# A hybrid attention, convolution and mixture-of-experts layer: router steps, output weights, gated sums and two norms are put in another order and on other engines

## The chip, the cores and the metric

The kernel runs on one core of a Trainium2 chip. The core has five engines that work side by side and wait for each other through semaphores: TensorE (PE, matrix products into PSUM), VectorE (DVE), ScalarE (ACT), GpSimd (POOL) and SyncE (SP, which issues most DMAs). Each engine takes its instructions strictly in the order in which they stand. The metric is the device time of one execution in microseconds; less is better.

## The reference, cut to what matters

One layer for 2048 tokens of 1024 features in float32:

```python
proj = x @ w_in                       # q, k, v, conv cb/cc/ch, two gates
attn = stick_breaking_attention(q, k, v)          # 8 heads of 64
branch_a = attn @ w_branch_a
branch_b = short_gated_conv(cb, cc, ch, conv_w) @ w_branch_b
gates = sigmoid(gate_logits + gate_bias)
mixed = (gate_a * branch_a + gate_b * branch_b) @ w_out
h = layer_norm(ALPHA * x + mixed, ln1_g, ln1_b)
ffn = hierarchical_moe(h)   # router: top 1 of 4 groups, top 2 of its 8 experts; SwiGLU experts
out = layer_norm(ALPHA * h + ffn, ln2_g, ln2_b)
```

## The kernel before

Products in float32 are made of three products of rounded halves: a tensor is split into a high part (ScalarE, line 103, `split`) and a low part (VectorE or GpSimd subtracts the high part, line 109), and TensorE runs high x high, high x low, low x high. So almost every weight passes through ScalarE and VectorE.

The program runs in stages. Projections and attention fill the first half (line 168 and lines 291 to 336). Then, for groups of 512 tokens in the order 2, 3, 0, 1, come `branches` and `mix_norm`.

`branches` (line 471) runs eight steps m for a group. A step loads 512 KB of branch weights (`raw`, line 480) and 512 KB of gates (`gt`, line 485, two buffers), splits the weights into `wh` and `wl`, and runs 24 matmuls of 512 columns into two PSUM tiles `ps_p` (line 490; two buffers in all). VectorE multiplies each PSUM tile by its gate (line 493), GpSimd adds the two halves (line 494), and the sum is split into `mh` and `ml`, eight of which are kept for a group.

`load_wo` (line 548) loads one of eight 512 KB rows of the output weights and splits it; the odd ones have their low part on GpSimd. Their raw tiles share four buffers named `r` with other tiles. The eight loads are written behind group 2's branches, and a scheduler that works ahead of time places them.

`mix_norm` (line 578) multiplies by the output weights (lines 589 to 591), adds the residual (592) and calls `layer_norm` (433): statistics on VectorE (423, 424), a power on GpSimd (427), and then either three instructions on ScalarE, GpSimd and VectorE (439 to 441) or, "at once", two on VectorE (436, 437). Before, only the last tile of all is done at once.

`router` transposes a normed tile (607), splits it (`ht`) and multiplies it by the router's weights (612). `choose` ranks a group's tokens: transposes of the logits (639), some thirty small VectorE instructions, a prefix sum (674, 675), one-hot rows on GpSimd (451) and columns on VectorE (452), and products of both (711). TensorE's order is written out by hand up to here: the generator `branches` yields once per matmul, and the group loop runs a step of the router or of `choose` at fixed counts k of these yields, 0 to 191, of the next group. The other engines' orders are the scheduler's.

After the experts (lines 770 to 900) the second norm runs over 16 tiles of 128 tokens: loads of 512 KB (1136), then for each pair of tiles statistics, a power (427), and ScalarE, GpSimd and VectorE instructions (1170 to 1172), and for one pair two VectorE instructions a tile (1167, 1168). The gain `g2` is kept in SBUF and in PSUM, the bias `b2` in PSUM.

Of the kernel before, what the change touches and what calls it, by code (L numbers as in the profile page):

```python
# [26 lines left out]
NT = S // P  # L27
# [4 lines left out]
ALPHA = 2.0 ** 0.25  # L32
EPS = 1e-5
# [23 lines left out]
def tile_hybrid_layer(  # L57
# [40 lines left out]
    def f32(t):  # L98
        return t.bitcast(F32)
# [316 lines left out]
    def norm_scales(pool, rows, eps, shift=True):  # L416

        n = len(rows)
        mv = pool.tile([P, n, 2], F32, name="mv", bufs=LEAD + 2)
# [5 lines left out]
        rs = pool.tile([P, n, 2], F32, name="rs", bufs=LEAD + 2)  # L425
# [42 lines left out]
    ph_b1, ph, ph_w = ExitStack(), ExitStack(), ExitStack()  # L468
    bq = open_pool(ph_b1, "bq", 1, side="right")

    def branches(n, outs):
        ah = bq.tile([P, 2, 4, G], F32R, name="ah")
        yh = bq.tile([P, 2, 4, G], F32R, name="yh")
        for t, src in ((ah, a_d), (yh, y_d)):
            for b in range(4):
                nc.sync.dma_start(f32(t)[:, :, b, :], src[b][n].rearrange("t p f -> p t f"))
        yield PAUSE_2
        for m in range(8):
            raw = bq.tile([P, NC, P], F32, name="raw", bufs=2)
            nc.sync.dma_start(raw, w_ab[m])  # L480
            wh = bq.tile([P, NC, P], F32R, name="wh", bufs=2)
            wl = bq.tile([P, NC, P], F32R, name="wl", bufs=2)
            split(wh, wl, raw)
            gt = bq.tile([P, 2, G], F32, name="gt", bufs=2)
            nc.sync.dma_start(gt, g_d[m][n].rearrange("s p f -> p s f"))
            for s, src in ((0, ah), (1, yh)):
                ps = ps_p.tile([P, G], F32, name="ps_p")
                for c in range(4):
                    for k, (a, b) in enumerate(((wh, 0), (wh, 1), (wl, 0))):
                        nc.tensor.matmul(ps, lhsT=a[:, 4 * s + c, :], rhs=src[:, b, c, :],  # L490
                                         start=(c == 0 and k == 0), stop=(c == 3 and k == 2))
                        yield G
                nc.vector.tensor_tensor(gt[:, s, :], gt[:, s, :], ps, op=ALU.mult)
            nc.gpsimd.tensor_tensor(gt[:, 0, :], gt[:, 0, :], gt[:, 1, :], op=ALU.add)
            h = bq.tile([P, G], F32R, name="mh", bufs=8)
            l = bq.tile([P, G], F32R, name="ml", bufs=8)
            split(h, l, gt[:, 0, :])
            outs.append((h, l))

    br_2 = []  # L500
    mixed(late, branches(2, br_2), RATE_3)
    run(late)
    ph_at.close()

# [34 lines left out]
    if True:  # L539
# [40 lines left out]
        def mix_norm(n, i, mh, ml):  # L580
            t = n * 4 + i
            tk = slice(i * P, (i + 1) * P)
            r = bp.tile([P, D], F32, name="r", bufs=4)
            nc.sync.dma_start(r, x[t * P:(t + 1) * P, :])
            for f in range(2):
                fs = slice(f * G, (f + 1) * G)
                ps = ps_b.tile([P, G], F32, name="ps_b")
                for c in range(NC):
                    nc.tensor.matmul(ps, lhsT=mh[c][:, tk], rhs=wo_h[:, c, fs], start=(c == 0), stop=False)
                    nc.tensor.matmul(ps, lhsT=mh[c][:, tk], rhs=wo_l[:, c, fs], start=False, stop=False)  # L590
                    nc.tensor.matmul(ps, lhsT=ml[c][:, tk], rhs=wo_h[:, c, fs], start=False, stop=(c == NC - 1))
                nc.vector.scalar_tensor_tensor(r[:, fs], r[:, fs], ALPHA, ps, op0=ALU.mult, op1=ALU.add)
                if f == 0:
                    yield None
            layer_norm(bp, r, g1, b1, r, EPS, n == GROUPS[-1] and i == 3)
            nc.sync.dma_start(h_d[t * P:(t + 1) * P, :], r)
            nc.sync.dma_start(acc_d[t * P:(t + 1) * P, :], r)
            yield r
# [31 lines left out]
        def choose(t0, nt, lt):  # L630
# [73 lines left out]
            for h in range(0, 2 * nt, 4):  # L704
                hs = range(h, min(h + 4, 2 * nt))
                c1 = bp.tile([P, 4, 3, 2 * NE], F32R, name="r", bufs=4)
                for a in hs:
                    one_hots(r1[:, a, :], c1[:, a % 4], row[:, a:a + 1], col[:, a:a + 1], tva[:, a, :],
                             nc.vector if t0 // 4 == GROUPS[-1] else nc.gpsimd)
                for a in hs:  # L710
                    nc.tensor.matmul(ps_tab[:, 0:6 * NE], lhsT=r1[:, a, :], rhs=c1[:, a % 4],
                                     start=(t0 == 4 * GROUPS[0] and a == 0), stop=(t0 == 4 * GROUPS[-1] + 2 and a == 3))
                yield

        for c in range(NC):
# [412 lines left out]
    with ExitStack() as ph:  # L1128
# [22 lines left out]
                                 start=True, stop=True)  # L1151
        g2 = fp.tile([P, D], F32, name="g2", bufs=1)
        nc.scalar.activation(g2, g2_ps, AF.Copy)
        scales = {}
        for u in range(0, NT + 2 * LEAD, 2):
            if u < NT:
                load_rows(2)
                scales[u] = norm_scales(fp, rows[u:u + 2], EPS / ALPHA ** 2, u not in AT_ONCE)
            t = u - 2 * LEAD
            if t < 0:  # L1160
                continue
            pair, at_once = rows[t:t + 2], t in AT_ONCE
            mv, rs = scales[t]
            for k, r in enumerate(pair):
                o = fp.tile([P, D], F32, name="o")
                if at_once:
                    nc.vector.scalar_tensor_tensor(r, r, mv[:, k, 0:1], g2, op0=ALU.subtract, op1=ALU.mult)
                    nc.vector.scalar_tensor_tensor(o, r, rs[:, k, 0:1], b2, op0=ALU.mult, op1=ALU.add)  # L1168
                else:
                    nc.scalar.activation(r, r, AF.Identity, bias=rs[:, k, 1:2], scale=rs[:, k, 0:1])  # L1170
                    nc.gpsimd.tensor_tensor(r, r, g2, op=ALU.mult)
                    nc.vector.tensor_tensor(o, r, b2, op=ALU.add)  # L1172
                nc.sync.dma_start(out[(t + k) * P:(t + k + 1) * P, :], o)
# [45 lines left out]
```

## Time and profile before

| what | value |
|---|---|
| median of three runs (lowest, highest) | 2606.8 us (2599.53, 2611.36) |
| the profiled execution, its own time | 2614.91 us |
| its span in the trace | 2613.2 us |
| granted TensorE clock, mean over the span | 0.973 |
| TensorE busy with matmuls | 94% |
| VectorE, ScalarE, GpSimd busy | 69%, 52%, 37% |
| DMA read and written | 394.5 MB, 104.4 MB |

A share of busy time is a mean over the whole span. Where a stage could be shorter is read from the rows of that stage: which engine stands idle there, and what ended its wait. An interval in brackets behind a row of the timeline is the engine's idle time just before it, with the instruction or transfer that ended it.

### The profile page before, as it was taken

The numbers are of one execution on the slowest core, as the hardware profiler recorded it, in microseconds if no ns is written. First come the engines' busy times: TensorE is split into PE (matmuls) and PEld (weight loads), VectorE is DVE, ScalarE is ACT, GpSimd is POOL, SyncE is SP. The second block draws the span as 40 slices with busy tenths as digits, with TensorE's granted clock in tenths as the row PEclk, the third lists the DMA queues.
The fourth block names the chain that finished last, engine by engine and source line by source line (L and its number), as shares of the span: only waits on it lengthen the run. The fifth ranks groups of instructions, "written<-read, shape, count | busy, mean of one in ns | idle before, by whom it ended". The sixth has DMA issues, their size and how long they took to land. (4 is left out here: it accounts for less than half of the span.)

```text
span 2613.2 us, 36756 instructions
## 1 busy us (share of the span) xinstructions
PE 2467.8 (94%) x12724; PEld 2079.0 (80%) x12724; DVE 1803.7 (69%) x2655; ACT 1363.2 (52%) x2334; POOL 975.7 (37%) x1323
## 2 busy tenths in 40 slices
PE   8999999999999999999989999959999999999981
PEld 7878888888888888888778778748988888888870
DVE  3257876577866567666766575578788878887848
ACT  3245565455555556555532122136677767777642
POOL 0033443254444444444532232313342443343336
PEclk9999999999999999999999999969999999999995
DMA  7433464423233335332573564257899989998967
GB/s 262 145 106 112 135 202 154 154 89 101 81 117 108 99 105 175 104 105 69 182 286 131 201 213 142 97 209 252 286 310 318 324 302 325 321 316 295 306 175 259
DMA packets 195120, 501.38 MB, mean 192 GB/s; under 512 B 19921, under 2 KB 44497, under 8 KB 194929
## 3 DMA queue, kind: packets, MB, share of 16 engines
q1 hardware_dynamic: 182962, 456.91, 50.7%
q0 software_dynamic: 11968, 42.08, 6.9%
q8 instruction: 101, 1.65, 0.3%
q14 instruction: 89, 0.73, 0.1%
HBM read 394.52 MB, written 104.40 MB: 191 GB/s over the span
## 5 line engine op out<-in xcount | busy, mean ns | idle before, releaser
L168 PE MATMUL ps_p<-xh,wh 128*128 128x512 f32 x1280 | 504.9, 394 | 8.0 <-ACT xh L103 6.6
L168 PE MATMUL ps_p<-xh,wl 128*128 128x512 f32 x1280 | 503.3, 393 | 0.0
L168 PE MATMUL ps_p<-xl,wh 128*128 128x512 f32 x1280 | 503.1, 393 | 0.1
L316 POOL TENSOR_TENSOR w<-w,pi 128x512 f32<-128x512 f32 (+2 forms) x256 | 300.4, 1174 | 222.7 <-DVE pi L311 221.7
L311 DVE TENSOR_TENSOR_SCAN pi<-z,cr,w 128x512 f32<-128x512 f32 x192 | 246.2, 1282 | 197.8 <-ACT z L298 188.4
L296 ACT ACTIVATE w<-z 128x512 f32<-128x512 f32 (+1 forms) x320 | 170.4, 532 | 359.9 <-PE z L291 324.4
L109 DVE TENSOR_TENSOR wlo<-wraw,whi 128x1024 fp32r<-128x1024 f32 x256 | 313.6, 1236 | 39.8 <-ACT whi L103 38.3
L882 PE MATMUL pg<-xt,whi 128*128 128x384 f32 (+2 forms) x1216 | 333.7, 354 | 4.7 <-DVE v L888 4.6
L103 ACT ACTIVATE whi<-wraw 128x1024 fp32r<-128x1024 f32 x256 | 268.5, 1056 | 73.8 <-DMA wraw<-in_w_gu 68.0
L884 PE MATMUL pg<-xt,wlo 128*128 128x192 f32 (+2 forms) x1216 | 295.0, 243 | 0.0
L168 PEld LDWEIGHTS ps_p<-xh,wh 128*128 128x128 f32 x1280 | 241.1, 188 | 58.7 <-ACT xh L103 6.6
L168 PEld LDWEIGHTS ps_p<-xl,wh 128*128 128x128 f32 x1280 | 241.0, 188 | 51.3 <-DVE xl L109 0.6
L168 PEld LDWEIGHTS ps_p<-xh,wl 128*128 128x128 f32 x1280 | 241.0, 188 | 51.1
L882 PEld LDWEIGHTS pg<-xt,whi 128*128 128x128 f32 x1216 | 230.7, 190 | 7.5 <-DVE v L888 6.5
L884 PEld LDWEIGHTS pg<-xt,wlo 128*128 128x128 f32 x1216 | 234.6, 193 | 0.8
L109 DVE TENSOR_TENSOR wl<-raw,wh 128x1024 fp32r<-128x1024 f32 x112 | 177.8, 1587 | 75.0 <-ACT wh L103 70.8
L336 PE MATMUL acc<-wt,vt 128*128 128x512 f32 (+3 forms) x640 | 207.2, 405 | 1.7 <-DVE wt L109 1.0
L109 DVE TENSOR_TENSOR wt<-pt,wt 128x512 fp32r<-128x512 f32 (+1 forms) x320 | 188.1, 589 | 28.6 <-ACT wt L103 28.3
L103 ACT ACTIVATE wh<-raw 128x1024 fp32r<-128x1024 f32 x112 | 118.6, 1059 | 140.8 <-PE ps_p L168 84.9
L291 PE MATMUL z<-kt,qs 128*128 128x512 f32 (+3 forms) x640 | 180.7, 364 | 1.5 <-ACT stay L298 0.9
L109 DVE TENSOR_TENSOR dlo<-draw,dhi 128x1024 fp32r<-128x1024 f32 x96 | 117.2, 1235 | 93.7 <-ACT dhi L103 93.5
L103 ACT ACTIVATE dhi<-draw 128x1024 fp32r<-128x1024 f32 x128 | 132.6, 1056 | 90.4 <-DMA draw<-in_w_dn 60.9
(250 smaller groups left out, 4952.2 us busy)
## 6 DMA issues: line engine op xcount, KB each, us to landing
wraw<-in_w_gu SPq DMA_DIRECT2D x256, 512.0 KB, 6.8
draw<-in_w_dn SPq DMA_DIRECT2D x124, 512.0 KB, 6.9
raw<-in_w_in SPq DMA_DIRECT2D x80, 512.0 KB, 3.9
kt<-k_d SPq DMA_DIRECT2D x96, 256.0 KB, 3.9
g_d<-t SPq DMA_DIRECT2D x64, 256.0 KB, 2.0
raw<-in_w_ab SPq DMA_DIRECT2D x32, 512.0 KB, 3.5
gt<-g_d SPq DMA_DIRECT2D x32, 512.0 KB, 4.3
vt<-v_d SPq DMA_DIRECT2D x48, 256.0 KB, 3.2
```

The costliest lines, as they stand in the source:

```text
L103: nc.scalar.activation(hi, src, AF.Copy)
L109: eng.tensor_tensor(lo, src, f32(hi), op=ALU.subtract)
L168: nc.tensor.matmul(ps, lhsT=a[:, c, :], rhs=b[:, c, :], start=(c == 0 and k == 0), stop=(c == NC - 1 and k == 2))
L291: nc.tensor.matmul(z[:, lo:], lhsT=qs[:, i * P:(i + 1) * P], rhs=kt[:, t, lo:], start=(t == 0), stop=(t == 1))
L296: nc.scalar.activation(w[:, lo:], z[:, lo:], AF.Sigmoid, scale=DH ** -0.5)
L311: nc.vector.tensor_tensor_scan(pi[:, lo + 1:], stay[:, lo:], (stay if diag else w)[:, lo:], first, op0=ALU.mult, op1=ALU.bypass)
L316: eng.tensor_tensor(w[:, lo:], w[:, lo:], pi[:, lo:G], op=ALU.mult)
L336: nc.tensor.matmul(acc[:, 0:nq * P], lhsT=kv[h, kc][1][:, b, :], rhs=wt[:, s, 0:nq * P], start=(kc == j and b == 3 and s == 0), stop=(kc = ...
L882: nc.tensor.matmul(pg[:, 0:2 * cap], lhsT=wh[:, c, :], rhs=xt[:, c, :, :], start=(c == 0), stop=False)
L884: nc.tensor.matmul(pg[:, cap:2 * cap], lhsT=wl[:, c, :], rhs=xt[:, c, 0, :], start=False, stop=(c == NC - 1))
```

## The change

Five edits. The router's steps go to other counts k (8, 30, 42, 54, 132, 144, 168, 184 in place of 48, 66, 84, 150, 172, 188, and one that was run at once), and the one-hot rows are made a step earlier than their products. The split of branch weights of step m must stand behind the gate product of step m - 2 on its engines, and load c of the output weights behind the gate load of step c and the low part of step c - 1; all their low parts go to VectorE. The sum of the two gated halves goes from GpSimd to VectorE. The last tile of every group is normed at once. The second norm goes tile by tile, in four ways: statistics on VectorE ("v") or as two ScalarE sums ("s"), and the end on ScalarE, GpSimd and VectorE ("g") or on VectorE alone ("v").

```diff
@@ branches
+        merged = []
         for m in range(8):
...
-            split(wh, wl, raw)
+            with tc.issue_after(merged[-2].ins) if m > 1 else ExitStack():
+                split(wh, wl, raw)
             gt = bq.tile([P, 2, G], F32, name="gt", bufs=2)
-            nc.sync.dma_start(gt, g_d[m][n].rearrange("s p f -> p s f"))
+            asked = nc.sync.dma_start(gt, g_d[m][n].rearrange("s p f -> p s f"))
...
-                nc.vector.tensor_tensor(gt[:, s, :], gt[:, s, :], ps, op=ALU.mult)
-            nc.gpsimd.tensor_tensor(gt[:, 0, :], gt[:, 0, :], gt[:, 1, :], op=ALU.add)
+                gated = nc.vector.tensor_tensor(gt[:, s, :], gt[:, s, :], ps, op=ALU.mult)
+            merged.append(gated)
+            nc.vector.tensor_tensor(gt[:, 0, :], gt[:, 0, :], gt[:, 1, :], op=ALU.add)
...
-            split(h, l, gt[:, 0, :])
+            nc.scalar.activation(h, gt[:, 0, :], AF.Copy)
+            low = nc.vector.tensor_tensor(l, gt[:, 0, :], f32(h), op=ALU.subtract)
             outs.append((h, l))
+            if paced is not None:
+                paced.append((asked, low))
@@ load_wo, mix_norm, choose
-            split(wo_h[:, c, :], wo_l[:, c, :], raw, lo_eng="pool" if c % 2 else "dve")
+            split(wo_h[:, c, :], wo_l[:, c, :], raw)
...
-            layer_norm(bp, r, g1, b1, r, EPS, n == GROUPS[-1] and i == 3)
+            layer_norm(bp, r, g1, b1, r, EPS, i == 3)
...
+                yield
                 for a in hs:
                     nc.tensor.matmul(ps_tab[:, 0:6 * NE], lhsT=r1[:, a, :], rhs=c1[:, a % 4],
...
-                yield
+            yield
         for c in range(NC):
-            load_wo(c)
+            with tc.issue_after(paced[c][0].ins), tc.issue_after(paced[max(c - 1, 0)][1].ins):
+                load_wo(c)
@@ the group loop
-                    if k in (48, 66):
-                        next(waiting[0])
-                    elif k in (84, 150, 172, 188):
-                        next(waiting[1])
+                    if k in waiting:
+                        next(waiting[k])
...
-            next(rts[2])
             if n != GROUPS[-1]:
-                waiting = [rts[3], choose(4 * n, 4, lt)]
+                chosen = choose(4 * n, 4, lt)
+                waiting = {8: rts[2], 30: rts[3], 42: rts[3]} | {k: chosen for k in (54, 132, 144, 168, 184)}
@@ the second norm
+        WAYS = ("vg", "sg", "sv", "vg", "sg", "sv", "vg", "sg", "sv", "vg", "sg", "sv", "vg", "vv", "sv", "vv")
+        def moments(r, way):
+            m = fp.tile([P, 4], F32, name="m", bufs=8)
+            if way[0] == "v":
+                mv, rs = norm_scales(fp, [r], EPS / ALPHA ** 2, way[1] == "g")
+                return mv[:, 0, 0:1], ALU.subtract, rs[:, 0, 0:1], rs[:, 0, 1:2]
+            junk = fp.tile([P, D], F32, name="junk", bufs=2)
+            nc.scalar.activation(junk, r, AF.Copy, scale=-1.0 / D, accum_out=m[:, 0:1])
+            nc.scalar.activation(junk, r, AF.Square, bias=m[:, 0:1], accum_out=m[:, 1:2])
+            nc.gpsimd.tensor_scalar(m[:, 2:3], m[:, 1:2], 1.0 / D, EPS / ALPHA ** 2, op0=ALU.mult, op1=ALU.add)
+            nc.gpsimd.tensor_tensor(m[:, 2:3], m[:, 2:3], mhalf, op=ALU.pow)
...
-        for u in range(0, NT + 2 * LEAD, 2):
+        for u in range(NT + 2 * LEAD):
...
+            if WAYS[t][1] == "v":
+                nc.vector.scalar_tensor_tensor(r, r, mean, g2_ps, op0=less, op1=ALU.mult)
+                nc.vector.scalar_tensor_tensor(o, r, scale, b2, op0=ALU.mult, op1=ALU.add)
+            else:
+                nc.scalar.activation(r, r, AF.Identity, bias=shift, scale=scale)
+                nc.gpsimd.tensor_tensor(r, r, g2, op=ALU.mult)
+                nc.vector.tensor_tensor(o, r, b2, op=ALU.add)
```

VectorE in the branches of group 2, steps 3 and 4, before (`gt` gated product, `wl` low part of branch weights, `ml` low part of the sum, `wo_l` low part of output weights, with buffer numbers; the `wo_l` of odd rows is on GpSimd and the sum too):

```order
L493 TENSOR_TENSOR gt_13384<-gt_13384,ps_p_13386 128x512
L493 TENSOR_TENSOR gt_13384<-gt_13384,ps_p_13400 128x512
L109 TENSOR_TENSOR wl_13463<-raw_13460,wh_13462 128x1024
L109 TENSOR_TENSOR ml_13416<-gt_13384,mh_13415 128x512
L109 TENSOR_TENSOR wo_l_13637<-r_13690,wo_h_13636 128x1024
L493 TENSOR_TENSOR gt_13425<-gt_13425,ps_p_13427 128x512
L493 TENSOR_TENSOR gt_13425<-gt_13425,ps_p_13441 128x512
```

The same place now:

```order
L497 TENSOR_TENSOR gt_13384<-gt_13384,ps_p_13386 128x512
L497 TENSOR_TENSOR gt_13384<-gt_13384,ps_p_13400 128x512
L109 TENSOR_TENSOR wo_l_13637<-r_13678,wo_h_13636 128x1024
L499 TENSOR_TENSOR gt_13384<-gt_13384 128x512
L109 TENSOR_TENSOR wl_13463<-raw_13460,wh_13462 128x1024
L497 TENSOR_TENSOR gt_13425<-gt_13425,ps_p_13427 128x512
L503 TENSOR_TENSOR ml_13416<-gt_13384,mh_13415 128x512
L109 TENSOR_TENSOR wo_l_13637<-r_13682,wo_h_13636 128x1024
L497 TENSOR_TENSOR gt_13425<-gt_13425,ps_p_13441 128x512
```

The sum (L499) is new on VectorE, each step has one `wo_l`, and from step 4 on it stands between the two gated products of the step.

GpSimd from the first mixed group to the second, before (`rs` power, `r` times `g` the norm's gain, `gt` the gated sums, `r` from `i` the one-hot rows):

```order
L427 TENSOR_TENSOR rs<-rs,mhalf 128x1
L440 TENSOR_TENSOR r<-r,g_13638 128x1024
L494 TENSOR_TENSOR gt<-gt 128x512 x6
L451 TENSOR_SCALAR r<-i_13605,row 128x128 x8
L494 TENSOR_TENSOR gt<-gt 128x512 x2
```

And now:

```order
L440 TENSOR_TENSOR r<-r,g_13638 128x1024
L427 TENSOR_TENSOR rs<-rs,mhalf 128x1
L451 TENSOR_SCALAR r<-i_13605,row 128x128 x8
L427 TENSOR_TENSOR rs<-rs,mhalf 128x1
L440 TENSOR_TENSOR r<-r,g_13638 128x1024
```

The eight sums are gone from GpSimd, and of four products with the gain three are left. On TensorE the instructions are the same ones: between a group's last transposes (607) and the router's product on them (612) stand now 8 matmuls of the next group where there were none, between the prefix sum (675) and the first products of one-hots (711) 36 where there were 22, and between the logits' transposes (639) and the prefix sum 78 where there were 66.

## Rows read from the trace of the kernel before

**Rows 1.** The page's first part: busy time, share of the span, instructions.
```profile
PE 2467.8 (94%) x12724; PEld 2079.0 (80%) x12724; DVE 1803.7 (69%) x2655; ACT 1363.2 (52%) x2334; POOL 975.7 (37%) x1323
```

**Rows 2.** Stretches: length, busy us (instructions) per engine, granted clock, DMA share, GB/s.
```profile
1293.15:1349.73 56.58, 49.15 (x194) 39.21 (x192) 40.36 (x45) 21.25 (x26) 25.57 (x21) 0.91 0.80 275
1349.73:1452.86 103.13, 99.44 (x463) 81.60 (x462) 65.89 (x129) 25.55 (x37) 29.79 (x24) 0.98 0.50 181
1452.86:1555.11 102.25, 98.24 (x464) 80.50 (x462) 65.09 (x128) 24.24 (x36) 29.79 (x24) 1.00 0.51 185
1555.11:1656.77 101.66, 98.05 (x463) 80.55 (x462) 64.20 (x129) 23.18 (x34) 29.57 (x24) 1.00 0.48 171
2550.00:2613.00 63.00, 7.03 (x8) 2.33 (x8) 53.89 (x81) 17.63 (x15) 39.76 (x22) 0.50 0.75 267
```

**Rows 3.** Timeline of TensorE, group 2's branches: start, length, instruction, idle before.
```profile
1311.47 0.70 PE L490 MATMUL ps_p<-ah,wh 128*128 128x512 f32 x2 [1.82 <-DVE gt L493]
...
1321.99 0.70 PE L490 MATMUL ps_p<-ah,wh 128*128 128x512 f32 x2 [3.20 <-DVE gt L493]
...
1331.69 0.70 PE L490 MATMUL ps_p<-ah,wh 128*128 128x512 f32 x2 [2.40 <-DVE gt L493]
```

**Rows 4.** Timeline of VectorE in the same stretch.
```profile
1307.76 1.23 DVE L109 TENSOR_TENSOR wo_l<-r,wo_h 128x1024 fp32r<-128x1024 f32 x1
...
1310.63 1.29 DVE L493 TENSOR_TENSOR gt<-gt,ps_p 128x512 f32<-128x512 f32 x2 [0.92 <-DMA gt<-g_d]
...
1318.74 2.51 DVE L109 TENSOR_TENSOR wo_l<-r,wo_h 128x1024 fp32r<-128x1024 f32 x1 [0.81 <-ACT wo_h L103]
...
1327.53 3.41 DVE L109 TENSOR_TENSOR wo_l<-r,wo_h 128x1024 fp32r<-128x1024 f32 x1
```

**Rows 5.** Issue to landing, 1280 to 1372: output weights (line 550), then gates (485).
```profile
DMA to landing us min/median/max: 5.1/6.7/7.4
...
DMA to landing us min/median/max: 3.5/7.1/11.5
```

**Rows 6.** Groups by line, whole program, ScalarE: busy us, mean ns, idle before.
```profile
L103 ACT ACTIVATE wh<-raw 128x1024 fp32r<-128x1024 f32 x112 | 118.6, 1059 | 140.8 <-PE ps_p L168 84.9 <-PE ps_p L490 52.9 <-DMA raw<-in_w_in 3.0
L103 ACT ACTIVATE mh<-gt 128x512 fp32r<-128x512 f32 x32 | 20.2, 631 | 70.7 <-POOL gt L494 70.7
```

**Rows 7.** TensorE's waits, 1365 to 1690: us in total, times, longest.
```profile
PE ps_tab L711 <- POOL r L451: 5.2, 12, 0.7
PE pt L612 <- DVE ht L109: 3.7, 3, 1.2
PE pr_ps L675 <- DVE mc L671: 2.4, 3, 0.9
```

**Rows 8.** Timeline of TensorE around the first products of one-hots.
```profile
1443.94 0.36 PE L711 MATMUL ps_tab<-r 128*128 128x192 f32 x1 [0.45 <-POOL r L451]
...
1446.57 0.68 PE L490 MATMUL ps_p<-ah,wh 128*128 128x512 f32 x1
```

**Rows 9.** Groups by line, 1350 to 1657, VectorE and GpSimd.
```profile
L109 DVE TENSOR_TENSOR wl<-raw,wh 128x1024 fp32r<-128x1024 f32 x23 | 46.9, 2037 | 2.1 <-ACT wh L103 1.9
...
L451 POOL TENSOR_SCALAR r<-i,row 128x128 fp32r<-128x128 f32 x24 | 18.4, 781 | 11.3 <-PE ps_p L490 11.3
```

**Rows 10.** Groups by line, the second norm, 2548 to 2614.
```profile
L1171 POOL TENSOR_TENSOR r<-r,g 128x1024 f32<-128x1024 f32 x14 | 33.5, 2408 | 4.1 <-ACT r L1170 3.8
L423 DVE BATCH_NORM_STATS2 st<-r 128x6 f32<-128x512 f32 x32 | 20.3, 676 | 7.3 <-DMA r<-acc_d 7.3
L1172 DVE TENSOR_TENSOR o<-r,b 128x1024 f32<-128x1024 f32 x14 | 16.6, 1198 | 0.0
L1170 ACT ACTIVATE r<-r,rs 128x1024 f32<-128x1024 f32 x14 | 16.6, 1233 | 25.7 <-DVE rs L429 25.7
...
L429 DVE SCALAR_TENSOR_TENSOR rs<-mv,rs 128x2 f32<-128x2 f32 x7 | 6.0, 862 | 0.0
L1167 DVE SCALAR_TENSOR_TENSOR r<-r,mv,g 128x1024 f32<-128x1024 f32 x2 | 4.7, 2352 | 0.0
...
L1168 DVE SCALAR_TENSOR_TENSOR o<-r,rs,b 128x1024 f32<-128x1024 f32 x2 | 2.5, 1268 | 0.0
```

More of the change, by code (lines that the diff above doesn't have):

```diff
@@ L418, in norm_scales @@
         n = len(rows)
-        mv = pool.tile([P, n, 2], F32, name="mv", bufs=LEAD + 2)
+        mv = pool.tile([P, n, 2], F32, name="mv", bufs=2 * LEAD + 2)
         for k, r in enumerate(rows):
@@ L424, in norm_scales @@
             nc.vector.bn_aggr(mv[:, k, :], st)
-        rs = pool.tile([P, n, 2], F32, name="rs", bufs=LEAD + 2)
+        rs = pool.tile([P, n, 2], F32, name="rs", bufs=2 * LEAD + 2)
         nc.vector.tensor_scalar(rs[:, :, 0], mv[:, :, 1], eps, None, op0=ALU.add)
@@ L469, in tile_hybrid_layer, with branches @@
     bq = open_pool(ph_b1, "bq", 1, side="right")
-    def branches(n, outs):
+    def branches(n, outs, paced=None):
         ah = bq.tile([P, 2, 4, G], F32R, name="ah")
@@ L492, in branches @@
                         yield G
-                nc.vector.tensor_tensor(gt[:, s, :], gt[:, s, :], ps, op=ALU.mult)
-            nc.gpsimd.tensor_tensor(gt[:, 0, :], gt[:, 0, :], gt[:, 1, :], op=ALU.add)
+                gated = nc.vector.tensor_tensor(gt[:, s, :], gt[:, s, :], ps, op=ALU.mult)
+            merged.append(gated)
+            nc.vector.tensor_tensor(gt[:, 0, :], gt[:, 0, :], gt[:, 1, :], op=ALU.add)
             h = bq.tile([P, G], F32R, name="mh", bufs=8)
             l = bq.tile([P, G], F32R, name="ml", bufs=8)
-            split(h, l, gt[:, 0, :])
+            nc.scalar.activation(h, gt[:, 0, :], AF.Copy)
+            low = nc.vector.tensor_tensor(l, gt[:, 0, :], f32(h), op=ALU.subtract)
             outs.append((h, l))
-    br_2 = []
-    mixed(late, branches(2, br_2), RATE_3)
+            if paced is not None:
+                paced.append((asked, low))
+    br_2, paced = [], []
+    mixed(late, branches(2, br_2, paced), RATE_3)
     run(late)
@@ L719, in tile_hybrid_layer @@
         nc.sync.dma_start(acc_d[S:S + P, :], zero)
-        waiting = []
+        waiting = {}
         for n in GROUPS:
@@ L744, in tile_hybrid_layer @@
                 rts.append(router(i, r, lt))
-            next(rts[2])
             if n != GROUPS[-1]:
-                waiting = [rts[3], choose(4 * n, 4, lt)]
+                chosen = choose(4 * n, 4, lt)
+                waiting = {8: rts[2], 30: rts[3], 42: rts[3]} | {k: chosen for k in (54, 132, 144, 168, 184)}
         rest = choose(4 * n + 2, 2, lt)
-        for step in (rts[3], most, rts[3], most, rest, rest, rest):
+        for step in (rts[2], rts[3], most, rts[3], most, most, rest, rest, rest, rest):
             next(step)
@@ L1153, in tile_hybrid_layer @@
         nc.scalar.activation(g2, g2_ps, AF.Copy)
+        WAYS = ("vg", "sg", "sv", "vg", "sg", "sv", "vg", "sg", "sv", "vg", "sg", "sv", "vg", "vv", "sv", "vv")
[9 more added lines that the diff above has]
+            nc.gpsimd.tensor_tensor(m[:, 2:3], m[:, 2:3], mhalf, op=ALU.pow)
+            if way[1] == "g":
+                nc.gpsimd.tensor_tensor(m[:, 3:4], m[:, 0:1], m[:, 2:3], op=ALU.mult)
+            return m[:, 0:1], ALU.add, m[:, 2:3], m[:, 3:4]
         scales = {}
-        for u in range(0, NT + 2 * LEAD, 2):
+        for u in range(NT + 2 * LEAD):
             if u < NT:
-                load_rows(2)
-                scales[u] = norm_scales(fp, rows[u:u + 2], EPS / ALPHA ** 2, u not in AT_ONCE)
+                load_rows(u + 7 - len(rows))
+                scales[u] = moments(rows[u], WAYS[u])
             t = u - 2 * LEAD
@@ L1161, in tile_hybrid_layer @@
                 continue
[L1162 to L1173, printed above, removed]
+            r, (mean, less, scale, shift) = rows[t], scales[t]
+            o = fp.tile([P, D], F32, name="o")
+            if WAYS[t][1] == "v":
[5 more added lines that the diff above has]
+                nc.vector.tensor_tensor(o, r, b2, op=ALU.add)
+            nc.sync.dma_start(out[t * P:(t + 1) * P, :], o)
     if dbg is not None:
```

## The prediction

> **What bounds the kernel now.** I read the page's shares first, then the busy times by stretch, then for each stretch that the change touches the waits of its bounding engine. TensorE is busy for 94% of the span [rows 1], so a gain can only come from its idle time, from time at its lower clock, or from stages in which it doesn't set the pace. Three stages are touched, and their rows tell them apart [rows 2]: group 2's branches with the loads of the output weights (stage A, 56.58 us), the three mixed groups (stage B, 103.13, 102.25 and 101.66 us) and the second norm (stage C, 63.00 us). In A and B TensorE bounds; in C VectorE does, with 53.89 us of 63, beside DMAs at a share of 0.75. The projections, attention and experts keep their instructions, and I count nothing there.
>
> Stage A: TensorE is busy for 49.15 of 56.58 us, so 7.4 us are idle. They are three waits of 1.82, 3.20 and 2.40 us, all for a gated product `gt` on VectorE [rows 3]. The clock's mean is 0.91, and its levels are 1.0 and 0.5, so 56.58 x 0.09 / 0.5 = 10.2 us went by at the lower level, where half the work is lost: 5.1 us. A loses 12.5 us in all. VectorE delays `gt` because it works in order: ahead of it stands a `wo_l` that takes 1.23 us alone, but 2.51 and 3.41 us later in the stage, and one `gt` waits 0.92 us for its gates to land [rows 4].
>
> Stage B: TensorE waits for GpSimd's one-hot rows (5.2 us in 12 waits), for `ht` (3.7 in 3) and for `mc` (2.4 in 3) [rows 7]. The first figure is too small for what is lost there: from 1443.49, where the first wait begins, to 1446.57 stand eight products of 192 columns [rows 8]. An undisturbed step of 24 matmuls of 512 columns takes 9.70 us between two marked instructions, less the wait of 2.40 and one third of the clock's 5.1: 5.6 us [rows 3], or 0.23 a matmul. Eight of 192 columns are then 0.7 us, and 2.4 are lost a group, 7.2 in three. The first group shows a clock of 0.98 and is 1.5 us longer than the third [rows 2]. B can give back 7.2 + 3.7 + 2.4 + 1.5 = 14.8 us.
>
> **The change part by part.** *Output weights paced, gated sums on VectorE (A).* The sum (0.65 us a step, as a gated product: 1.29 for two [rows 4]) comes to VectorE, and so do the odd low parts; GpSimd has nothing large left in the stage. I price `wo_l` and `wl` at the 1.23 us of the one that ran alone [rows 4]. Load c is now asked for behind the low part of step c - 1, so there is a ring through two steps: landing L, high part 1.06 (the row of `wh`, same size [rows 6]), `wo_l` 1.23, gated product 0.65, `wl` 1.23, sum 0.65, `mh` 0.63 [rows 6], gated product 0.65, `ml` 0.65. That is L + 6.75 us for two steps, which TensorE needs in 2 x 5.6 = 11.2; it holds for L up to 4.5. Unpaced loads landed after 5.1 to 7.4 us, median 6.7, gates after 3.5 to 11.5 [rows 5]. With one load on the way at a time I take the smallest, 5.1: a step of 5.93, so 8 x 0.33 = 2.6 us late, of which the two PSUM buffers hide about 2. What follows: 0.6. Behind a `wo_l` that waits on VectorE are queued the second gated product, the sum and `ml`, for which TensorE's PSUM buffers wait. The first wait of 1.82 hangs on gates that landed late; a `wo_l` now stands ahead of that product too, so I let it grow by 0.85, a middle of 0 and 1.23 rounded up: 2.7 stay. Whether a lone wait of that size still lowers the clock I bound by 0 and 1.7, and take 0. A gains 12.5 - 3.3 = 9. Bounds: at L = 6.7 the step is 6.73, eight are 9.0 late, 7 after the buffers, and with 2.7 and a little of the clock the gain is 2; at best all 12.5 come back.
>
> *Router's steps, one-hots a step earlier, sums off GpSimd (B).* GpSimd's eight one-hots take 8 x 0.78 = 6.2 us [rows 9]. They had 22 matmuls (5.1 us) of cover and now 36 (8.3 us), with no gated sum in between: 7.2 us go. For `ht` 8 matmuls of the next group (1.9 us) now stand ahead of the product where there were none, against waits of 1.2 at most: 3.7 go. The wait for `mc` was 0.9 at most, and 12 more matmuls cover 2.8: 2.4 go. On VectorE eight sums (5.2 us) are added a group, and the last tile's two instructions come in place of one, 2.35 + 1.27 - 1.20 = 2.4 [rows 10]; against that `wl`, 2.04 us in the mean beside GpSimd's sums, falls towards 1.23: 23/3 x 0.81 = 6.2 less [rows 9]. So VectorE keeps about 82 of 102 us, and TensorE covers it; if that cover were gone, the 7.6 added a group would be the price. ScalarE's `mh` waited 70.7 us in all for GpSimd's sum [rows 6], which was off the path. I leave 1.8 us for new small waits: B gains 13. Bounds: 4, if only the clock's 1.5 and the waits for `mc` go, and 14.8.
>
> The Trainium skill ("SBUF — State Buffer", Who interferes with whom) says that a VectorE instruction with two inputs in SBUF and a GpSimd instruction that reads SBUF shut each other out for a whole instruction, and that one with a single SBUF input is free of it. That speaks against the sums on VectorE beside the three products with `g1` that stay on GpSimd, and for the pairs of stage C that read the gain from PSUM. The trace agrees: 2.35 us with gain in SBUF, 1.27 and 1.20 with an operand in PSUM [rows 10]. By the rule each product could hold a sum or a `wl` up for 2.4 us, which VectorE's free 20 us a group hold.
>
> *Second norm tile by tile (C).* Of 16 tiles 7 have statistics on VectorE (before 16): 9 x 2 x 0.676 = 12.2 us less. 9 instead of 14 adds: 5 x 1.20 = 6.0 less. The two-instruction end serves 7 tiles instead of 2. Its second instruction is known, 1.27; the first reads the gain from PSUM, which no row shows: between 1.20 (nearest: one input in PSUM) and 2.35 (gain in SBUF). I take 1.27: 7 x 2.54 - 2 x 3.62 = 10.5 more [rows 10]. VectorE: 53.9 - 7.7 = 46 us. At 2.35 it is 54, as before. ScalarE goes from 14 x 1.23 = 17 to (9 + 18) x 1.23 = 33 us, the sums priced as the instruction it has. GpSimd's products go from 33.5 to 9 x 2.41 = 22. The DMAs' share of 0.75 is 47 us at full use [rows 2], and loads ahead of the first tile and the last store add to it, so no more than about 10 can go. The 7.7 us are the most that VectorE gives; nine tiles now have a power (and more) on GpSimd behind a product of 2.41, which delays their end. Gain 5; bounds -11 (nine tiles late by half a product, 9 x 1.2, none of it hidden) and 10.
>
> Sum: 9 + 13 + 5 = 27 us. The profiled execution took 2614.9 us, its span is 2613.2, and it lies 8.1 above the median of 2606.8. On its own scale the changed kernel takes 2588; on the median's, in which I forecast, 2606.8 - 27 = 2580.
>
> **The rivals.** (a) The paced loads land late, L = 6.7, because gates and branch weights share the queues. For it: the median of the row, and gates at 7.1 [rows 5]; against it, fewer loads at a time. 2 + 13 + 5 = 20: 2587. (b) The second norm loses: ScalarE's sums stand in order ahead of the ends of other tiles, and powers wait behind products. For it: small instructions beside products are already slow, 862 ns for 128 x 2 elements [rows 10]; against it, every engine's total falls below 47. C = -6, so 16: 2591. (c) The steps only move their waits, since `ht` and one-hots are still made by engines in order. Against it: each cover exceeds its wait. 9 + 4 + 5 = 18: 2589. (d) All at its best, 12.5 + 14.8 + 10 = 37: 2569. (e) Slower, by the ring in stage A alone. At a landing of 13 us a step is 9.9 and seven steps are 30 us late; with 2 hidden and about 2 lost to the clock that eats the other 18 us of gain, and from there it is slower. At 16 us it is 11.4, seven are 41 late, A = -27: 2616. It needs a landing beyond the longest of any gate, 11.5 [rows 5].
>
> [...] The lower clock shows after the waits of stage A, and in only one of three like groups (0.98 against 1.00) [rows 2]. So the same waits need not bring it. [...] By it the median's runs may lack part of the 5.1 + 1.5 us that I count as given back, and the gain would be 27 - 6.6 = 20: 2586. It stands inside (a)'s time and has half of its chance.
>
> **How the numbers follow.** My case has 0.50, (a) and the clock together 0.17, (b) 0.13, (c) 0.07, (d) 0.08, (e) 0.05. My case's own range is 2572 to 2587 (each term off by a third). The range for 8 in 10 leaves out (e), the half of (d) beyond it and the worst of (b), where C nears -11: 2565 to 2598. About 0.5%, 13 us, is what a measurement of this kernel can tell from no change: below 2594 is faster, above 2620 slower. Faster: 0.49 + 0.14 + 0.07 + 0.05 + 0.08 = 0.83; slower: (e) where the landing is longer still, and (b) with (a), 0.04; the rest, 0.13, is the same.
>
> **What would show it.** Right: stage A of about 47.5 us at a clock of 0.98 or more, with one wait for `gt` above 1 us; groups of about 98 us without waits for one-hots, `ht` or `mc`; a first end instruction in the second norm near 1.27 us and that stage near 58 us. Wrong: regular waits for `gt` in A with VectorE waiting for `wo_h` (then L is the step that failed); VectorE above 90% in a group; ScalarE or GpSimd named by VectorE's waits in the second norm at every other tile.

## The result, and the profile after

The changed kernel takes 2580.6 us (median of five runs, 2577.2 to 2583.4), the kernel before 2604.8 in the same comparison (five runs, 2599.5 to 2611.4). The ratio is 0.9902, with a 95% interval of 0.9885 to 0.9920; in a later comparison it was 0.9906 (0.9885 to 0.9926). The forecast was 2580. The profiled execution took 2583.4 us with a span of 2581.7; its mean clock is 0.977.

The stretches of [rows 2] in the changed kernel, then the experts and what follows the last expert product (length, then busy us and instructions of PE, PEld, VectorE, ScalarE and GpSimd, clock, DMA share, GB/s):

```profile
1293.47:1340.69 47.22, 44.88 (x193) 35.58 (x192) 37.50 (x55) 20.92 (x25) 2.82 (x7) 1.00 0.85 290
1340.69:1441.11 100.42, 98.57 (x464) 81.56 (x462) 65.59 (x139) 24.97 (x36) 17.79 (x15) 0.98 0.57 206
1441.11:1539.95 98.84, 96.99 (x463) 80.37 (x462) 64.34 (x137) 23.38 (x34) 17.59 (x15) 1.00 0.53 189
1539.95:1640.25 100.30, 98.45 (x464) 81.59 (x462) 63.33 (x136) 22.31 (x33) 17.58 (x15) 0.98 0.49 176
1640.25:2516.68 876.43, 833.25 (x4867) 735.87 (x4865) 684.87 (x1086) 565.95 (x891) 312.24 (x163) 0.97 0.85 282
2516.68:2581.70 65.02, 7.79 (x10) 2.49 (x8) 42.74 (x58) 31.72 (x47) 33.69 (x39) 0.50 0.76 267
```

The last two of these stretches in the first profile of before:

```profile
1656.77:2541.26 884.49, 839.08 (x4867) 740.69 (x4865) 684.67 (x1085) 565.07 (x890) 315.64 (x164) 0.97 0.83 279
2541.26:2613.20 71.94, 7.61 (x10) 2.48 (x8) 54.81 (x83) 18.32 (x16) 41.33 (x23) 0.50 0.71 242
```

Between the two profiles the span falls by 31.5 us: 9.4 in stage A (56.58 to 47.22), 7.5 in the three groups (307.04 to 299.56), 8.1 in the experts, 6.9 after them, less 0.3 lost ahead of A. The experts' 8.1 are chance, as the second profile of before will show. Without them 23.4 remain, beside 24.2 by the medians.

Stage A in the changed kernel, TensorE's idle time above 0.3 us:

```profile
1311.65 0.70 PE L494 MATMUL ps_p<-ah,wh 128*128 128x512 f32 x2 [1.68 <-DVE gt L497]
...
1326.00 0.73 PE L494 MATMUL ps_p<-yh,wh 128*128 128x512 f32 x2 [0.32 <-DVE gt L497]
...
1337.82 0.73 PE L494 MATMUL ps_p<-yh,wh 128*128 128x512 f32 x2 [0.34 <-DVE gt L497]
```

Against [rows 3] the waits of 3.20 and 2.40 are gone, the first is 1.68 in place of 1.82, and the clock is 1.00. The ring of the prediction can be seen turning. SyncE asks for the loads:

```profile
1316.04 0.46 SPq L558 DMA_DIRECT2D r<-in_w_out  x1
...
1323.59 0.46 SPq L558 DMA_DIRECT2D r<-in_w_out  x1
...
1329.53 0.46 SPq L558 DMA_DIRECT2D r<-in_w_out  x1
```

ScalarE starts their high parts (in brackets how long it waited for the load):

```profile
1323.02 1.06 ACT L103 ACTIVATE wo_h<-r 128x1024 fp32r<-128x1024 f32 x1 [2.51 <-DMA r<-in_w_out]
...
1328.68 1.06 ACT L103 ACTIVATE wo_h<-r 128x1024 fp32r<-128x1024 f32 x1 [0.34 <-DMA r<-in_w_out]
...
1334.85 1.06 ACT L103 ACTIVATE wo_h<-r 128x1024 fp32r<-128x1024 f32 x1 [0.84 <-DMA r<-in_w_out]
```

VectorE, the same steps:

```profile
1324.12 1.23 DVE L109 TENSOR_TENSOR wo_l<-r,wo_h 128x1024 fp32r<-128x1024 f32 x1 [0.99 <-ACT wo_h L103]
1325.26 0.68 DVE L497 TENSOR_TENSOR gt<-gt,ps_p 128x512 f32<-128x512 f32 x1
...
1330.92 0.68 DVE L497 TENSOR_TENSOR gt<-gt,ps_p 128x512 f32<-128x512 f32 x1
...
1337.08 0.68 DVE L497 TENSOR_TENSOR gt<-gt,ps_p 128x512 f32<-128x512 f32 x1
```

From the asking to the high part pass 7.0, 5.1 and 5.3 us in these rows. Over the six loads that are asked for one by one it is 4.7 to 7.0, in the mean 5.7, and the askings stand 6.00 us apart in the mean. The two rounds shown, from gated product to gated product, take 5.66 and 6.16. Every `wo_l` has its 1.23 us again, where [rows 4] had 2.51 and 3.41.

In the groups the waits for `ht` and for one-hot rows [rows 7] are gone. A wait for `mc` has grown. TensorE at the prefix sum of the first group:

```profile
1422.88 0.33 PE L682 MATMUL pr_ps<-mm,tri 128*128 128x128 f32 x1 [0.35 <-DVE mm L674]
1424.71 0.33 PE L683 MATMUL pr_ps<-mc,ones 128*128 128x128 f32 x1 [1.51 <-DVE mc L679]
```

VectorE at that place:

```profile
1420.80 0.69 DVE L499 TENSOR_TENSOR gt<-gt 128x512 f32<-128x512 f32 x1
1421.40 1.22 DVE L109 TENSOR_TENSOR wl<-raw,wh 128x1024 fp32r<-128x1024 f32 x1
1422.54 0.28 DVE L674 TENSOR_TENSOR mm<-oh 128x128 fp32r<-128x128 f32 x1
...
1422.82 0.68 DVE L503 TENSOR_TENSOR ml<-gt,mh 128x512 fp32r<-128x512 f32 x1
1423.42 0.68 DVE L497 TENSOR_TENSOR gt<-gt,ps_p 128x512 f32<-128x512 f32 x1
1424.02 0.64 DVE L679 TENSOR_TENSOR mc<-mc,mm 128x32 fp32r<-128x32 f32 x3
```

VectorE doesn't idle here. TensorE reaches the prefix sum while `mm` is still behind the gated sum (L499, new on this engine) and `wl`, and `mc` behind a `ml` and the next gated product. The pair of waits (0.35 and 1.5) stands in each group, 5.55 us in all, in place of 2.4 for `mc` before.

Groups by line in the second norm after (busy us, mean ns, idle before), to be read beside [rows 10]:

```profile
L1199 POOL TENSOR_TENSOR r<-r,g 128x1024 f32<-128x1024 f32 x9 | 21.2, 2357 | 0.1
L1200 DVE TENSOR_TENSOR o<-r,b 128x1024 f32<-128x1024 f32 x9 | 10.8, 1194 | 1.5 <-POOL r L1199 1.5
...
L423 DVE BATCH_NORM_STATS2 st<-r 128x6 f32<-128x512 f32 x14 | 9.0, 681 | 9.8 <-DMA r<-acc_d 9.8
L1196 DVE SCALAR_TENSOR_TENSOR o<-r,m,b 128x1024 f32<-128x1024 f32 x5 | 6.3, 1267 | 0.0
L1195 DVE SCALAR_TENSOR_TENSOR r<-r,m,g_ps 128x1024 f32<-128x1024 f32 x5 | 6.3, 1265 | 0.2 <-ACT junk L1177 0.2
...
L1179 POOL TENSOR_TENSOR m<-m,mhalf 128x1 f32<-128x1 f32 x9 | 4.9, 552 | 0.5
```

The instruction that no row showed, a gain read from PSUM, takes 1.27 us. VectorE is busy for 42.7 us in place of 54.8.

### The profile page after: what moved, and what is told of

It reads as the page before. It is cut to its first block, busy times and chain, and to the rows that moved or that the text cites. A ratio compares the mean times of both kernels' runs of the same rounds, so it can differ in the third digit from the quotient of the medians.

```text
span 2581.7 us, 36732 instructions
## 1 busy us (share of the span) xinstructions
PE 2456.1 (95%) x12724; PEld 2071.6 (80%) x12724; DVE 1786.9 (69%) x2666; ACT 1375.2 (53%) x2362; POOL 908.8 (35%) x1300
## 5 line engine op out<-in xcount | busy, mean ns | idle before, releaser
L109 DVE TENSOR_TENSOR wl<-raw,wh 128x1024 fp32r<-128x1024 f32 x112 | 155.2, 1386 | 73.6 <-ACT wh L103 63.1
```

The costliest lines, as they stand in the source:

```text
L109: eng.tensor_tensor(lo, src, f32(hi), op=ALU.subtract)
```

## The experiments

Stage lengths of every profile, us (A: first matmul of group 2's branches to the first product of the output weights; groups: from there to the same product of the next group, three times; experts: from the last group's first such product to the last expert product; end: from there to the last instruction). The last column has the ratio of the times, where a kernel ran more than once:

| kernel | A | groups | experts | end | ratio to before |
|---|---|---|---|---|---|
| before | 56.58 | 103.13 102.25 101.66 | 884.5 | 71.9 | |
| before, again | 56.95 | 103.18 102.25 101.74 | 875.9 | 72.5 | |
| changed | 47.22 | 100.42 98.84 100.30 | 876.4 | 65.0 | 0.9902 |
| changed, again | 47.89 | 100.43 99.02 99.03 | 873.7 | 64.7 | 0.9906 (0.9885 to 0.9926) |
| no pacing | 49.66 | 100.38 100.32 99.00 | 875.5 | 64.3 | 0.9901 (0.9874 to 0.9929) |
| odd low parts on GpSimd | 50.03 | 101.30 98.83 99.01 | 874.1 | 65.0 | one run |
| sums on GpSimd | 50.52 | 98.57 100.18 101.92 | 881.8 | 64.4 | 0.9918 (0.9891 to 0.9945) |
| last tile on three engines | 47.93 | 99.77 99.81 101.19 | 879.2 | 64.9 | one run |
| old second norm | 48.60 | 98.87 99.99 98.85 | 876.1 | 72.1 | 0.9942 (0.9922 to 0.9962) |
| gain from SBUF | 46.24 | 98.88 99.01 99.02 | 880.4 | 66.8 | one run |
| prefix sum later | 46.31 | 97.98 97.93 97.90 | 874.8 | 65.0 | 0.9884 (0.9857 to 0.9911) |
| and products later | 48.13 | 97.53 97.48 97.00 | 879.1 | 64.6 | 0.9877 (0.9854 to 0.9901) |
| and pacing by own step | 45.41 | 98.23 97.49 97.00 | 878.1 | 66.1 | 0.9890 (0.9869 to 0.9911) |

What a stage varies by with its own order untouched is read from the columns: A 46.2 to 48.6 in seven profiles (mean 47.5), the groups' sum 296.9 to 299.7 in five (both of the changed kernel, no pacing, old norm, gain from SBUF), experts 873.7 to 884.5, end 64.3 to 66.1 in the nine with the new norm as it is. A difference below that is nothing.

**The kernel before, again.** No edit.

> The kernel before once more, for a second profile of it. The stretch from the last mixed group's end to the last expert product took 884.5 us before and 876.4 after, though its instructions are the same; kernels with the change took 875 to 882. Theory (chance: single waits of ScalarE and VectorE and the clock behind them differ from run to run): 874 to 882 here, so nothing of the change's gain is in this stretch. Rival (the change gives something back here, by what it leaves behind): 883 us or more again. The other stages within 1 us of 56.6, 103.1, 102.3, 101.7 and 71.9.

The experts took 875.9 us; A, groups and end repeat within 0.6. So the 8.1 us between the first two profiles are no gain of the change: the first profile of before was a long one.

**No pacing.**

```diff
-            with tc.issue_after(paced[c][0].ins), tc.issue_after(paced[max(c - 1, 0)][1].ins):
-                load_wo(c)
+            load_wo(c)
```

> The changed kernel with the eight output weight loads no longer held to the branches' steps; all low parts stay on VectorE and the gated sums too. Ring theory (pacing keeps wo_l from standing ahead of gated products in pairs): the loads bunch into steps 2 to 4, three of which each carry two or three wo_l (1.23 us each) beside 5.6 us of TensorE work, so group 2's branches take 51 to 55 us instead of 47.2, with two or three waits for gt over 1 us, and the whole 4 to 8 us more. Rival (what cost time before was GpSimd beside VectorE, not the bunching): the stage stays at 47 to 49 us.

A took 49.66, between the two. There is one long wait, of 2.96, at the place where the changed kernel waits 1.68. TensorE, then VectorE, there:

```profile
1312.60 0.77 PE L494 MATMUL ps_p<-ah,wh 128*128 128x512 f32 x1 [2.96 <-DVE gt L497]
```

```profile
1308.90 1.23 DVE L109 TENSOR_TENSOR wo_l<-r,wo_h 128x1024 fp32r<-128x1024 f32 x1 [1.50 <-ACT wo_h L103]
1310.04 0.68 DVE L503 TENSOR_TENSOR ml<-gt,mh 128x512 fp32r<-128x512 f32 x1
1310.64 1.22 DVE L109 TENSOR_TENSOR wo_l<-r,wo_h 128x1024 fp32r<-128x1024 f32 x1
1311.78 1.28 DVE L497 TENSOR_TENSOR gt<-gt,ps_p 128x512 f32<-128x512 f32 x2
```

Bunched low parts stand ahead of a gated product, but at 1.23 us each they cost one long wait and no more. Pacing is worth about 2 us of the 9 (49.66 is 1.1 to 3.4 above the seven), and not visible in the time (0.9901). Neither theory had it: the ring theory asked for two or three waits and 51 us or more.

**Odd low parts on GpSimd.**

```diff
-            split(wo_h[:, c, :], wo_l[:, c, :], raw)
+            split(wo_h[:, c, :], wo_l[:, c, :], raw, lo_eng="pool" if c % 2 else "dve")
```

> The changed kernel with the low parts of the odd output weight rows back on GpSimd, still paced, sums on VectorE. Theory (what stage A lost before came from GpSimd working beside VectorE: wo_l of 2.51 and 3.41 us): wo_l or wl beside GpSimd's subtractions takes 2 us or more, and the branches of group 2 take 49 to 52 us, two or more above the 47.2 to 48.6 of the changed order. Rival (pacing and the moved sums are enough, and VectorE has less to do): 46 to 48 us.

A took 50.03, within the theory's range. GpSimd, VectorE and ScalarE at the longest wait (TensorE, 3.05 us, before 1333.29):

```profile
1329.73 2.35 POOL L109 TENSOR_TENSOR wo_l<-r,wo_h 128x1024 fp32r<-128x1024 f32 x1 [10.96 <-ACT wo_h L103]
```

```profile
1330.21 2.42 DVE L503 TENSOR_TENSOR ml<-gt,mh 128x512 fp32r<-128x512 f32 x1 [3.37 <-ACT mh L502]
1332.56 0.67 DVE L497 TENSOR_TENSOR gt<-gt,ps_p 128x512 f32<-128x512 f32 x1
```

```profile
1328.60 1.06 ACT L103 ACTIVATE wo_h<-r 128x1024 fp32r<-128x1024 f32 x1 [5.63 <-DMA r<-in_w_out]
1329.56 0.61 ACT L502 ACTIVATE mh<-gt 128x512 fp32r<-128x512 f32 x1
```

Two things add up. ScalarE, in order, holds `mh` behind a `wo_h` that waited 5.63 us for its load, so `ml` is 3.37 late; then `ml`, 0.68 us elsewhere, takes 2.42 and ends 0.55 behind GpSimd's instruction: it ran after it. The gated product for which TensorE waits stands behind both. The company costs 1.7 of the 3.05 directly. The victim was `ml`, not the `wo_l` or `wl` that the theory named, and the theory had nothing of the late load, so this one run doesn't settle the shares.

**Sums on GpSimd.**

```diff
-            nc.vector.tensor_tensor(gt[:, 0, :], gt[:, 0, :], gt[:, 1, :], op=ALU.add)
+            nc.gpsimd.tensor_tensor(gt[:, 0, :], gt[:, 0, :], gt[:, 1, :], op=ALU.add)
```

> The changed kernel with the gated sums back on GpSimd, everything else as changed. Theory (on VectorE the sum spares a pass to GpSimd and back, and spares wl and the one-hots the company of GpSimd): wl in the groups goes back from about 1.2 to 2 us, the one-hots wait behind sums again, and the three groups lose 1 to 3 us each; group 2's branches stay near 48 us since nothing else of size is on GpSimd there. Whole: 3 to 8 us more than the changed kernel. Rival (VectorE relieved of 5.2 us a group brings mm and mc forward): the waits for mc shrink from 1.5 to below 0.9 and the groups get no longer.

A took 50.52, not the 48 of the theory, with one long wait (2.99) and a mean clock of 0.93. Four of VectorE's subtractions there (`wl`, `wo_l`) take 1.9 to 2.3 us in place of 1.22. The groups took 300.7 in place of 298.5 and 299.6, for another reason than the theory's. TensorE's waits in the three groups:

```profile
PE ps_b L597 <- ACT mh L502: 5.9, 3, 2.6
```

The waits for `mm` and `mc` are gone entirely, as the rival said: the sums on VectorE are what made them late. What comes in their place is a late `mh` of a group's last step. GpSimd, then VectorE, ahead of the second of these waits (2.34 us, before 1449.10):

```profile
1430.55 7.39 POOL L451 TENSOR_SCALAR r<-i,row 128x128 fp32r<-128x128 f32 x8 [2.63 <-PE ps_p L494]
1437.91 2.53 POOL L499 TENSOR_TENSOR gt<-gt 128x512 f32<-128x512 f32 x2
```

```profile
1444.85 1.28 DVE L497 TENSOR_TENSOR gt<-gt,ps_p 128x512 f32<-128x512 f32 x2 [3.02 <-DMA gt<-g_d]
```

Two sums stand behind the eight one-hots. The gates of the last step need the buffer of the first of them, so they are asked for late (1441.02), and the last gated products wait 3.02 us for them; the last sum then takes 2.12 us on GpSimd. The wait of the first group, 0.94, has no one-hots ahead of it. A and the groups together take 351.2 us, against 343.2 to 346.8 in the four profiles with all of the changed order in both. So the sum on VectorE pays on balance, though it brought its own wait.

**Last tile on three engines.**

```diff
-            layer_norm(bp, r, g1, b1, r, EPS, i == 3)
+            layer_norm(bp, r, g1, b1, r, EPS, n == GROUPS[-1] and i == 3)
```

> The changed kernel with the last tile of a group normed on three engines again, as before. Theory (VectorE is the engine that makes mm and mc late): with 2.4 us less on it a group, the wait for mc falls from 1.5 us to below 1 or stays, and no wait for ht comes, since 8 and 30 matmuls of cover stand there: the groups take 0 to 1 us less each. Rival (the longer way over ScalarE and GpSimd makes the last tile's logits late): waits for ht or for the ranking, 0.5 to 2 us a group more.

```profile
PE pr_ps L683 <- DVE mc L679: 4.5, 3, 1.5
PE pt L615 <- DVE r L441: 1.9, 3, 0.7
```

The waits for `mc` stay at 1.5 although VectorE has less to do, and a new one of 0.65 a group appears at the tile's transposes. The rival held: this part of the change saves about 0.65 us a group.

**Prefix sum later.**

```diff
-                waiting = {...} | {k: chosen for k in (54, 132, 144, 168, 184)}
+                waiting = {...} | {k: chosen for k in (54, 144, 152, 172, 188)}
```

> The changed kernel with the last four steps of choose at 144, 152, 172 and 188 instead of 132, 144, 168 and 184. Theory (the prefix sum's mc is late by its place on VectorE, behind the next gated product, and 12 more matmuls, 2.7 us, pass that place): the waits for mm (0.35) and mc (1.5) go in all three groups, the groups come to about 97.5 us each (from 100.42, 98.84, 100.30), the lower clock goes with them, and the whole is 5 to 8 us less. Rival 1 (the order on VectorE is made anew around it and mc stays just late): no change. Rival 2 (28 matmuls in place of 36 before the first products are too few for eight one-hots of 0.78 us): waits of 0.3 to 0.5 us for the one-hots come back, 3 us of the gain are lost.

The groups took 97.98, 97.93 and 97.90 at a clock of 1.00, all waits for `mm` and `mc` gone, and all that is left of idle time is the second rival's:

```profile
PE ps_tab L720 <- POOL r L451: 2.5, 6, 0.4
```

VectorE's order up to `mc` stayed the same; TensorE came 12 matmuls later. The sum of 293.8 is 3.1 to 5.9 below the five profiles with the changed groups, and 3.1 below the one of them whose clock is 1.00 in all three groups (gain from SBUF, 296.9): as much as the waits fell, from 5.55 to 2.5. With the products at 176 and 190:

> The changed kernel with the last four steps of choose at 144, 152, 176 and 190 instead of 132, 144, 168 and 184: the prefix sum's place that took the waits for mm and mc away, and the products four and two matmuls later than in that run, since their one-hots still came 0.4 us late twice a group. Theory (cover counted from the actual one-hots): the last 0.8 us a group go, groups take about 97.1 us each, and the whole is 5 to 8 us below the changed kernel. Rival (the products now crowd the group's end): new waits at the first product of the output weights, groups of 98 us, 3 to 5 us below the changed kernel.

```profile
1340.85:1438.38 97.53, 96.97 (x463) 80.58 (x462) 65.32 (x139) 25.61 (x36) 17.70 (x15) 1.00 0.59 212
```

The groups (the first is shown) sum to 292.0 us, 15.0 below before, 6.5 to 7.6 below the two profiles of the changed kernel and 4.9 below the lowest of the five; idle are 0.3 to 0.6 us a group. The times agree in size (2578.2 against 2583.5 in the same comparison), though the intervals of the ratios, 0.9877 and 0.9906, overlap.

**Pacing by the own step**, on top of that.

```diff
-            with tc.issue_after(paced[c][0].ins), tc.issue_after(paced[max(c - 1, 0)][1].ins):
+            with tc.issue_after(paced[c][0].ins), tc.issue_after(paced[min(c, 6)][1].ins):
```

> As the run with steps at 144, 152, 176 and 190, and each output weight load held behind the low part of its own step instead of the step before (the last two as they were nearly), so that wo_l stands ahead of both gated products of a step. Theory (the first wait of group 2's branches comes from two wo_l that stand ahead of one gated product): that wait of 1.5 to 2 us falls below 0.7 and the branches take 45 to 46.5 us. Rival (the ring is longer by a step's half, and wo_l waits for its load ahead of both products): waits of 0.5 to 1.5 us in each of five steps, branches of 48 to 52 us.

A took 45.41, less than in any other profile, yet not for the theory's reason: the first wait stays at 1.56, and the small ones behind it (0.3 to 0.6) are gone. Two `wo_l` still stand ahead of the first late gated product, so the theory on the cause of that wait stays untested. In the whole time nothing can be told (0.9890).

**Old second norm.** The loop over pairs of the diff's left side, all else as changed.

> The changed kernel with the second norm of before (pairs, one pair at once with the gain in SBUF). If the second norm gave what the two traces differ by from the last expert product to the end (71.94 against 65.02 us), this is 7 us slower than the changed kernel, 2587 or so, and that stretch is 71 to 73 us. Rival (the stretch is set by where the experts leave the DMAs, so part of the 6.9 is from elsewhere): 2 to 4 us slower and a stretch of 67 to 69 us.

The end took 72.1 us, and the whole 0.9942: the new second norm gives 7 us by itself.

**Gain from SBUF.**

```diff
-                nc.vector.scalar_tensor_tensor(r, r, mean, g2_ps, op0=less, op1=ALU.mult)
+                nc.vector.scalar_tensor_tensor(r, r, mean, g2, op0=less, op1=ALU.mult)
```

> The changed kernel with the gain of the second norm's two-instruction ends read from SBUF in place of PSUM. Theory: beside GpSimd's products the first instruction takes 2.0 to 2.4 us in place of 1.27, VectorE is busy for 47 to 50 us in place of 42 from the first load on, and the stretch from the last expert product takes 2 to 6 us more than 65.0. Rival (VectorE has room there, so it is hidden): the instruction takes as long but the stretch stays within 1 us of 65.0.

```profile
L1179 POOL TENSOR_TENSOR m<-m,mhalf 128x1 f32<-128x1 f32 x9 | 7.9, 881 | 0.6
L1195 DVE SCALAR_TENSOR_TENSOR r<-r,m,g 128x1024 f32<-128x1024 f32 x5 | 7.4, 1475 | 0.0
```

The end takes 66.8 us, 1.8 to 2.5 above eight profiles of the new norm; the ninth reached 66.1, so how much of this is the edit's is open. VectorE's instruction takes 1.48 in the mean, not 2.0 to 2.4; GpSimd's power goes from 552 to 881 ns. GpSimd's busy time rises from 33.7 to 39.6 us, VectorE's from 42.7 to 43.4. So the two engines shut each other out, and here GpSimd does most of the waiting. GpSimd, then VectorE, at two places:

```profile
2542.26 1.54 POOL L1179 TENSOR_TENSOR m<-m,mhalf 128x1 f32<-128x1 f32 x1
...
2560.80 4.67 POOL L1199 TENSOR_TENSOR r<-r,g 128x1024 f32<-128x1024 f32 x2
```

```profile
2542.13 1.26 DVE L1195 SCALAR_TENSOR_TENSOR r<-r,m,g 128x1024 f32<-128x1024 f32 x1
...
2564.29 2.26 DVE L1195 SCALAR_TENSOR_TENSOR r<-r,m,g 128x1024 f32<-128x1024 f32 x1
```

The power of 1.54 us started 0.13 behind VectorE's instruction and ended 0.41 after it. VectorE's instruction of 2.26, the only slow one of the five, started 1.18 before the end of a product and ended 1.08 after it. The Trainium skill ("SBUF — State Buffer", Who interferes with whom) says that the order of issue decides which of the two is blocked. These rows agree: each time the one that started later took longer.

## Why the prediction was right, point by point

**Stage A: 9 forecast, 9.4 measured, 8.0 to 10.3 over all profiles of that order.** The two waits above 2 us went and the clock came back, as forecast. The ring was right in its mean and not in its terms: a step of 5.93 was forecast and the askings stand 6.00 apart, but the landing was put at 5.1 and is 5.7 in the mean, up to 7.0, for which the prediction's own sum makes a step of 6.2. The small waits were put at 0.6 and are 0.32 and 0.34. The first wait was put at 2.7 and is 1.68. What the prediction didn't say is how much each part is worth: undone alone, pacing, odd low parts and sums cost 2 to 3 us each against the mean of 47.5, and about 9 came together. With all low parts and sums on VectorE and the output weights not paced A is already down to 49.7. That speaks for GpSimd's company, more than the bunching, as what was lost before; it doesn't show it, since the hold on the split of the branch weights, another part of the change, was undone in no run.

**Groups: 13 forecast, 7.5 measured (8.6 with the second profile after, 7.3 to 10.1 over the five).** The one-hots' and `ht`'s waits went as worked out. The step that failed is "12 more matmuls cover 2.8: 2.4 go". Cover was counted in TensorE's matmuls between the ranking and the prefix sum, while the same change puts 0.69 us of sum a step on the engine that makes `mm` and `mc`, in order, ahead of them. The prediction had those 5.2 us a group and set them against TensorE as a whole, not against this wait. The waits are 5.55 us in place of 2.4, a loss of 3.1 where 2.4 of gain stood: 5.5 us in all. The 1.8 left for new small waits cover part of that, and the clock took from the rest: with it at 1.00 in all three groups (gain from SBUF) the groups gave 10.1. With the prefix sum 12 matmuls later and the products moved too, the groups give 15.0, near the 14.8 us that the rows of before showed as lost.

A second slip had no consequence: the prediction read 81 us of VectorE's busy time a group out of [rows 2], but that column is TensorE's weight loads. VectorE had 66 and has 65.6. The clock's 1.5 us did not come back reliably either: the lower mean of 0.98 stands in two groups of the first profile after and in one of the second. It stands in no group of the three profiles with a later prefix sum, but in one with the sums on GpSimd, where the waits are for `mh`.

**Second norm: 5 forecast, 6.9 measured, 7 with the old norm put back.** Statistics, adds and ends came out as counted: 20.3 to 9.0, 16.6 to 10.8, 7.2 to 17.6. Left out were VectorE's small instructions behind the statistics (L424, L426 and L429), which fall from 13.7 to 7.0 us. The chosen price of 1.27 for the unseen instruction was exact.

**The sum.** 27 us were forecast and 24.2 came. The hit within 1 us is in part luck: the median of before moved from 2606.8 to 2604.8 with two more runs, and the second norm's 1.9 too little stands against the groups' 5.5 too much. Of the rivals, (a) had its late loads (three of the eight took 6.6 to 7.0 us) but not their price, since A gained 9.4 and not 2; (b) went the other way; (c) was right for one of the three waits. The way by the lower clock came in part, in the groups.

## What to carry to other kernels

Count cover on the engine that makes the operand, in its own order, with every instruction that the same change adds ahead of it; matmuls between two steps of TensorE say nothing of that. A late operand is then best met by asking for it later: 12 matmuls of distance gave the groups 3 to 6 us, with 2.5 of waits for one-hots already taken off. Two profiles of one kernel repeat the stages with fixed order within 0.7 us, and within 1.3 where the clock differs, so a stage's length tells an effect of 2 us that the whole time hides; a stage that runs through chance waits, as the experts here, must be profiled twice before its difference is believed.

## What the runs showed of the hardware that was not expected

With both operands in SBUF a VectorE instruction took 2.42 us, where 0.68 is usual, beside a GpSimd instruction of 2.35. In the second norm the same contention fell on GpSimd's small powers (552 to 881 ns) and spared VectorE's large instruction (1.27 to 1.48 in the mean, where 2.35 had been seen before). The clock answered the same wait differently. At the wait of 1.5 us for `mc`, or just behind it, the clock fell in 7 of the 21 groups that have this wait, and such a group took about 1.4 us more than its likes. In the first profile after, the mean from 1426.0 to 1429.0 is 0.50, and 1.00 from 1526.3 to 1529.3, at the same place of the next group. A stage's clock must also be looked up by place. The second profile after has 0.97 in stage A, but the lower stretch (0.50 from 1293.1 to 1296.1) stands at A's first matmuls, behind a wait of 0.96 us that every profile has there, and not behind A's own first wait, which ends at 1313.06 with 1.00 behind it.
